# Gate blocks of a hybrid attention layer: bank copies on ScalarE in place of VectorE

## The chip, the cores and the metric

The kernel runs on one core of a Trainium2 chip. A core has a matmul engine (TensorE, "PE" in the profile, its weight loads "PEld"), VectorE ("DVE"), ScalarE ("ACT"), GpSimd ("POOL") and SyncE ("SP"). Each engine takes its instructions from its own queue in the order in which the program was built; semaphores make one engine wait for another. Matmul results land in PSUM, eight banks of 128 partitions by 512 float32 words, and have to be copied out of a bank by DVE or ACT before the bank can be written anew. The metric is the device time of one execution in microseconds (us), the median of several runs.

## The reference, cut to what matters

One layer of a streaming encoder over a prompt of 1024 tokens and a sample of 32 new tokens with 512 cached ones; the kernel handles both as 1056 columns. One projection of the normalised input gives everything that the two attention branches and their gates need:

```python
p = h @ w_in      # 1024 -> 384 + 256 + 32 + 3*512 + 1024 + 1024
q_lat, c_kv, k_r, q_b, k_b, v_b, g_a, g_b = jnp.split(p, IN_SPLITS, axis=-1)
...
def sb_attend(q, qpos, k, v, kpos):            # branch B, stick-breaking, 8 heads of 64
    z = jnp.einsum('bqhd,bshd->bhqs', q, k).astype(jnp.float32) * SB_SCALE
    mask = kpos[None, :] < qpos[:, None]
    sp = jnp.where(mask, jax.nn.softplus(z), 0.0)
    later = lax.cumsum(sp, axis=3, reverse=True) - sp
    a = jnp.where(mask, jnp.exp(jax.nn.log_sigmoid(z) - later), 0.0)
    return jnp.einsum('bhqs,bshd->bqhd', a.astype(v.dtype), v)
...
merged = (jax.nn.sigmoid(g_a) * (o_a @ w_proj_a)
          + jax.nn.sigmoid(g_b) * (o_b @ w_proj_b))
```

Branch A (latent attention with softmax), the output projection and a convolutional feed-forward block follow. The change concerns the projections `g_a` and `g_b`, 2 x 1024 columns, which are computed early, put away in DRAM, and read back when the two branches are merged.

## The kernel before

Products are kept at float32 accuracy by splitting each operand into a high part and a rest and adding three products (`mm3`, L66: the lines L68 to L70 are its matmuls, high by high, rest by high and high by rest as the profile names them). `hi` (L61, on ACT) makes the high part, `lo` (L64, on DVE) the rest. Weights are loaded by `wload` (L77, issued on SP) and split by `wsplit`.

The stage in question is `stage_sb`. It goes through four pairs of heads. For a pair, `sb_pair` projects queries, keys and values (`mtile`: a block of output columns, 352 at a time, is 24 matmuls into one bank), then runs `attend` for each of the two heads. After each pair, `gates` projects four of the sixteen gate blocks of 128 rows, each in three blocks of 352 columns. A gate block's bank (tag `mm`, two banks in turn) is copied to a tile `nat` (two buffers in turn), and GpSimd's queue issues the store to the DRAM tensor `gd` (L649). That makes 48 copies (L648) and 48 stores.

In `attend`, 128 rows of queries at a time go through a chain that changes engines often:

- PE: scores into one or two banks of tag `s`, three banks in turn (L462 to L466);
- `sb_weights`: ACT takes Abs, Exp and Ln of each piece (L481, L482, L483), DVE makes softplus (L484), then a scan along the row, which is the reversed running sum (L486), then subtracts it from the scores (L489), which frees the `s` banks; ACT takes the last Exp (L490);
- PE transposes the weights 128 by 128 into a bank `tr` (L542); ACT splits off the high part (L61, tiles `PTh` and `ptd`), DVE the rest (L64, `PTl` and `ptd`);
- PE multiplies them with the values into a bank `pv` (L555); ACT copies one half (L559), DVE adds the other (L560), and the result is stored (L564).

The gate matmuls do not depend on the attention around them. The order of the instructions on each engine is not the order in which the Python code issues them: the framework's scheduler lays it out when the program is built, from dependencies, free buffers and its own estimates of durations, and mixes gate matmuls between the steps of attention. On the chip this order is fixed. Between gate blocks there are also small products for the modulation vectors (`ada_step`, L199 and L203), which use the same two `mm` banks.

Of the kernel before, what the change touches and what calls it, by code (L numbers as in the profile page):

```python
# [40 lines left out]
class K:  # L41
# [598 lines left out]
    def gates(self, ms):  # L640
        nc = self.nc
        for m in ms:
            wh, wl = self.w_in_tile(2208 + m * P)
            if self.ada_todo:
                self.ada_step(2, self.W, self.At)
            for c0, n, ps in self.mtile(wh, wl, self.Hh, self.Hl, self.BLK, KT):
                g = self.tl(self.At, [P, 512], F32, "nat")
                nc.vector.tensor_copy(g[:, :n], ps[:, :n])  # L648
                nc.gpsimd.dma_start(self.gd[m, :, c0 : c0 + n], g[:, :n])  # L649

    def att_pools(self):
# [930 lines left out]
    def stage_down(self):  # L1582
# [57 lines left out]
        def product(banks, s, weights, first, more=None, part=range(6)):  # L1640
            for i, (j, n) in enumerate(steps):
                if i not in part:
                    continue
                wh, wl = weights(i, j, n)
                gh, gl = gates(s, j, n)
                if more:
                    more(i, j, n)
                for k in range(n):
                    for t in range(4):
                        tk = slice(t * P, t * P + P)  # L1650
                        add3(banks[t], gh[:, k, tk], gl[:, k, tk], wh[:, k], wl[:, k], first and j + k == 0, j + k == NJ - 1)
# [189 lines left out]
```

## Time and profile before

| | us |
|---|---|
| median of three runs | 1797.5 |
| the three runs | 1796.99, 1797.5, 1802.86 |
| the profiled execution | 1796.74 |
| its span in the profile | 1794.7 |
| PE busy | 1733.5 (97%) |
| PEld busy | 1547.7 (86%) |
| DVE busy | 1258.4 (70%) |
| ACT busy | 1005.4 (56%) |
| POOL busy | 253.3 (14%) |
| DVE, the 48 copies L648 | 24.5 |

How the rows of the profile are read. A row of a group gives the line, the engine, the operation, output<-input by the program's names, shapes, and a count. A row of waits reads "who, line <- who released it, line: us in total, times, longest". A row of a stretch of time gives start:end and length, then busy us and number of instructions of PE, PEld, DVE, ACT and POOL, then the granted clock of PE as a share of full speed, the share of the DMA engines that is busy, and GB/s. A row of the time line gives start and length in us, then the instruction (x2: two in a row merged), and in brackets the idle time before it with what ended it. Matmuls overlap: a matmul of 352 columns has a mean length of some 330 ns in the groups, while the next one starts well before its end.

### The profile page before, as it was taken

To read this page: it belongs to the slowest core of one execution; us is meant where nothing else is said; L and a number is where in the kernel's file an instruction comes from. 1 tells how busy PE (TensorE), PEld (TensorE's weight loads), DVE (VectorE), ACT (ScalarE), POOL (GpSimd) and SP (SyncE) were. 2 spreads that over 40 slices of the span, in tenths; PEclk is the share of its full clock that TensorE was granted. 3 is DMA by queue.
4 is the path that set the end of the run, shared out by engine and by line. 5 is a ranking of instruction groups with operands and counts; after the bars stand their busy time and mean duration, and the time that the engine had idled before them with its cause. 6 is when DMAs were issued, how large, how long until landed. Compare 5 with 4: busy or idle time off the path is not lost. (4 is left out here: it accounts for less than half of the span.)

```text
span 1794.7 us, 30062 instructions
## 1 busy us (share of the span) xinstructions
PE 1733.5 (97%) x11610; PEld 1547.7 (86%) x11610; DVE 1258.4 (70%) x2087; ACT 1005.4 (56%) x1926; POOL 253.3 (14%) x518
## 2 busy tenths in 40 slices
PE   6999999999999999999999999999999999999997
PEld 3988888988888998888888868999999999977876
DVE  4677377576487467777676768977777787788446
ACT  4565366564464469688687357644444454544332
POOL 2112111110111001101000022321111111110001
PEclk9999999999999999999999999999999999999999
DMA  8333332332333112313336542333333323597426
GB/s 316 109 101 106 101 100 74 90 111 83 101 103 85 57 54 77 90 51 95 101 115 218 169 154 83 124 124 124 101 124 126 132 90 124 196 344 260 147 87 224
DMA packets 181710, 227.52 MB, mean 127 GB/s; under 512 B 13349, under 2 KB 129776, under 8 KB 181568
## 3 DMA queue, kind: packets, MB, share of 16 engines
q1 hardware_dynamic: 166048, 182.10, 31.7%
q0 software_dynamic: 15296, 43.42, 6.8%
q8 instruction: 91, 1.49, 0.3%
q14 instruction: 51, 0.42, 0.1%
q10 hardware_dynamic: 224, 0.09, 0.0%
HBM read 174.32 MB, written 51.25 MB: 126 GB/s over the span
## 5 line engine op out<-in xcount | busy, mean ns | idle before, releaser
L61 ACT ACTIVATE wh<-wr 128x1024 fp32r<-128x1024 f32 (+6 forms) x185 | 149.5, 818 | 254.9 <-PE s L1305 83.4
L64 DVE TENSOR_TENSOR wl<-wr,wh 128x1024 fp32r<-128x1024 f32 (+6 forms) x185 | 168.3, 916 | 137.0 <-ACT wh L61 135.5
L68 PE MATMUL mm<-hh,wh 128*128 128x352 f32 x696 | 229.6, 330 | 2.4 <-DVE nat L648 2.4
L69 PE MATMUL mm<-hl,wh 128*128 128x352 f32 x696 | 228.6, 328 | 0.4 <-DVE hl L277 0.4
L70 PE MATMUL mm<-hh,wl 128*128 128x352 f32 x696 | 228.0, 328 | 0.0
L68 PEld LDWEIGHTS mm<-hh,wh 128*128 128x128 f32 x696 | 131.3, 189 | 10.3 <-issue 4.1
L69 PEld LDWEIGHTS mm<-hl,wh 128*128 128x128 f32 x696 | 131.5, 189 | 2.7 <-DVE hl L277 0.9
L70 PEld LDWEIGHTS mm<-hh,wl 128*128 128x128 f32 x696 | 131.6, 189 | 1.2 <-issue 0.4
L542 PE MATMUL tr<-c,A 128*128 128x128 f32 x576 | 93.7, 277 | 4.9 <-ACT A L490 3.6
L1306 PE MATMUL s<-T,wl 128*128 128x256 f32 (+1 forms) x328 | 93.4, 285 | 0.0
L1305 PE MATMUL s<-T,wh 128*128 128x256 f32 (+1 forms) x328 | 93.3, 285 | 0.0
L1304 PE MATMUL s<-T,wh 128*128 128x256 f32 (+1 forms) x328 | 93.3, 284 | 0.0
L486 DVE TENSOR_TENSOR_SCAN A<-A 128x128 f32<-128x128 f32 (+8 forms) x66 | 87.8, 1343 | 0.4
L1442 DVE SCALAR_TENSOR_TENSOR u<-u,c,u 128x1058 f32<-128x1058 f32 x68 | 87.0, 1316 | 1.4 <-ACT u L1439 0.2
L490 ACT ACTIVATE A<-A 128x128 f32<-128x128 f32 (+8 forms) x66 | 44.6, 682 | 74.8 <-DVE A L489 74.3
L64 DVE TENSOR_TENSOR PTl<-tr,PTh 128x512 fp32r<-128x512 f32 x96 | 62.9, 683 | 29.9 <-ACT PTh L61 29.5
L542 PEld LDWEIGHTS tr<-c,A 128*128 128x128 f32 x576 | 67.5, 141 | 14.4 <-ACT A L490 8.1
L1304 PE MATMUL tr<-T,wh 128*128 128x272 f32 (+1 forms) x272 | 77.7, 286 | 0.0
L1306 PE MATMUL tr<-T,wl 128*128 128x272 f32 (+1 forms) x272 | 77.4, 285 | 0.0
L1305 PE MATMUL tr<-T,wh 128*128 128x272 f32 (+1 forms) x272 | 77.3, 284 | 0.0
L64 DVE TENSOR_TENSOR wl<-S,wh 128x1024 fp32r<-128x1024 f32 x40 | 48.9, 1223 | 37.8 <-ACT wh L61 37.8
L1304 PE MATMUL mm<-T,wh 128*128 128x256 f32 (+1 forms) x256 | 73.1, 286 | 0.0
(650 smaller groups left out, 5557.1 us busy)
## 6 DMA issues: line engine op xcount, KB each, us to landing
wr<-in_w_ada_dram SPq DMA_DIRECT2D x48, 512.0 KB, 4.7
wr<-in_w_up_dram SPq DMA_DIRECT2D x44, 512.0 KB, 3.8
dr<-in_w_down_dram SPq DMA_DIRECT2D x43, 512.0 KB, 5.8
wr<-gdn SPq DMA_DIRECT2D x34, 512.0 KB, 3.9
wr<-in_w_in_dram SPq DMA_DIRECT2D x33, 512.0 KB, 4.2
gdn<-u POOLq DMA_DIRECT2D x23, 512.0 KB, 4.8
gd<-nat POOLq DMA_DIRECT2D x48, 176.0 KB, 2.1
t<-gd SPq DMA_DIRECT2D x16, 528.0 KB, 5.2
```

The source lines that it names most:

```text
L61: self.nc.scalar.activation(out, in_, AF.Identity, scale=scale)
L64: return self.nc.vector.tensor_tensor(out, full, hi.bitcast(F32), ALU.subtract)
L68: m(ps, lh, rh, start=start, stop=False)
L69: m(ps, lh, rl, start=False, stop=False)
L70: m(ps, ll, rh, start=False, stop=stop)
L486: nc.vector.tensor_tensor_scan(r, r, r, 0.0, ALU.add, ALU.bypass)
L490: nc.scalar.activation(A[:, :w], A[:, :w], AF.Exp)
L542: nc.tensor.transpose(tr[:, (2 * s + q) * P : (2 * s + q + 1) * P], at[q][:, b * P : b * P + P], self.idt)
L1304: m(ps[:, :n], w[0][:, k], x[0][:, k, c], start=first and k == 0, stop=False, skip_group_check=True)
L1305: m(ps[:, :n], w[0][:, k], x[1][:, k, c], start=False, stop=False, skip_group_check=True)
L1306: m(ps[:, :n], w[1][:, k], x[0][:, k, c], start=False, stop=k == 3, skip_group_check=True)
L1442: nc.vector.scalar_tensor_tensor(y, u[:, w : w + YW], self.cvT[:, w, cc : cc + 1], y, ALU.mult, ALU.add)
```

## The change

One line in `gates`: the copy of a gate block out of its bank is issued on ScalarE and no longer on VectorE. Shape, source, target and store stay the same. As the scheduler lays out the order anew, the built program also differs in the order of instructions on all five queues, from the first gate copies to the end of `stage_sb`; ahead of that and behind it the order is the same.

```diff
             for c0, n, ps in self.mtile(wh, wl, self.Hh, self.Hl, self.BLK, KT):
                 g = self.tl(self.At, [P, 512], F32, "nat")
-                nc.vector.tensor_copy(g[:, :n], ps[:, :n])
+                nc.scalar.copy(g[:, :n], ps[:, :n])
                 nc.gpsimd.dma_start(self.gd[m, :, c0 : c0 + n], g[:, :n])
```

## The prediction, made before the change was run

> **What bounds the kernel now.** I read the page first, then sums by stretch, then the waits of the matmul engine in the stretch that the change touches, and last its time line around single waits.
>
> ```profile
> span 1794.7 us, 30062 instructions
> PE 1733.5 (97%) x11610; PEld 1547.7 (86%) x11610; DVE 1258.4 (70%) x2087; ACT 1005.4 (56%) x1926; POOL 253.3 (14%) x518
> ...
> 60.00:561.00 501.00, 486.01 (x3189) 431.30 (x3188) 330.57 (x545) 285.99 (x593) 75.24 (x131) 1.00 0.32 97
> ...
> 60.00:80.00 20.00, 20.00 (x128) 19.70 (x127) 8.57 (x13) 8.68 (x16) 3.06 (x4) 1.00 0.26 80
> 260.00:280.00 20.00, 19.64 (x131) 17.90 (x129) 18.45 (x31) 15.21 (x33) 2.18 (x4) 1.00 0.33 103
> ```
>
> TensorE (PE) is busy 97% of the span. The gate copies run from 93 to 561 us, so the second part of the fence is the stage that counts: in its 501 us PE is busy 486.0, the granted clock is 1.00, VectorE (DVE) has 330.6 us of work and ScalarE (ACT) 286.0. PE idles 15.0 us there, 0.8% of the kernel. That is the most that any relief of the other engines can win, unless the matmuls themselves shrink, which they do not. The last row shows why the other engines still matter: where attention is dense, DVE is busy 18.45 of 20 us, ACT 15.21. The row above it gives the pace of the gate matmuls alone: 128 in 20 us, 0.156 us each, so a block of 24 takes 3.75 us.
>
> The 15 us of idle time, by what ended them:
>
> ```profile
> PE s L462 <- DVE A L489: 7.2, 20, 1.0
> PE tr L542 <- ACT A L490: 2.7, 5, 0.7
> PE mm L68 <- DVE nat L648: 2.4, 2, 1.2
> PE pv L555 <- DVE PTl L64: 1.2, 4, 0.4
> PE pv L555 <- ACT PTh L61: 1.1, 2, 0.9
> ...
> PEld s L462 <- DVE A L489: 10.7, 18, 0.8
> PEld tr L542 <- ACT A L490: 7.0, 15, 1.0
> ...
> ACT A L490 <- DVE A L489: 68.7, 27, 4.7
> DVE A L484 <- ACT A L483: 20.7, 22, 2.3
> ```
>
> All 33 waits sit in the chain of stick-breaking attention: scores (L462) wait for a bank that DVE's subtraction (L489) must leave, transposes (L542) wait for ACT's last Exp (L490), and twice a gate block waits for the gate copy itself (L648). In the last two rows the Exp waits for DVE far longer than DVE waits for ACT: in this chain DVE is the late one.
>
> **The change, part by part.** Removed from DVE and added to ACT are the same 48 copies of 128x352 out of PSUM. DVE's price has a row; ACT's comes from copies of the same shape from the same kind of bank that it does today.
>
> ```profile
> L648 DVE COPY nat<-mm x48: 496/511/525, 93.1 to 560.8; 128x352 f32<-128x352 f32 x48
> L446 ACT COPY big<-mm x12: 452/452/455, 73.4 to 469.2; 128x352 f32<-128x352 f32 x12
> L649 POOL DMA_DIRECT2D gd<-nat x48: 539/568/603, 93.9 to 561.6; - x48
> DMA to landing us min/median/max: 2.1/2.1/5.5
> ```
>
> DVE loses 48 x 0.510 = 24.5 us (330.6 becomes 306.1), ACT gains 48 x 0.452 = 21.7 us (286.0 becomes 307.7). Both stay some 193 us under the 501 of the stage, so neither becomes its bound, and these two terms add nothing by themselves. In ends and starts a copy costs DVE a little less, 0.42 us, since the next instruction starts before its end (below). The 48 stores stay on POOL's queue and follow the copy; POOL is busy 75 of 501 us, a store is issued in 0.57 us and lands in 2.1, 2.7 together, less than the 3.75 of a block, so the two copy buffers come free as before. A few stores of gates and of attention outputs change places on POOL's queue, and on SP's queue one cache load moves behind two weight loads; nobody on PE waits for these today, and I put them at nothing.
>
> In the built program the instructions are not only moved from one queue to the other: the scheduler lays the stage out anew. From the end of the stage on, all five queues are the same as before. So the effect is a matter of PE's waits between 60 and 561 us, and I go through them.
>
> Gain, first term: waits for the copy itself.
>
> ```profile
> 102.61 1.75 DVE L486 TENSOR_TENSOR_SCAN A<-A 128x768 f32<-128x768 f32 x1
> 104.27 0.50 DVE L648 COPY nat<-mm 128x352 f32<-128x352 f32 x1
> 104.68 1.01 DVE L489 TENSOR_TENSOR A<-s,A 128x384 f32<-128x384 f32 x2
> ...
> 104.82 0.43 PE L68 MATMUL mm<-hh,wh 128*128 128x352 f32 x1 [1.21 <-DVE nat L648]
> 366.24 0.43 PE L68 MATMUL mm<-hh,wh 128*128 128x352 f32 x1 [1.19 <-DVE nat L648]
> ...
> 105.73 0.85 ACT L490 ACTIVATE A<-A 128x768 f32<-128x768 f32 x1 [3.70 <-DVE A L489]
> ```
>
> The copy lay behind a scan of 1.75 us while ACT had nothing to do for 3.70 us. Both waits go: -1.21 - 1.19 = -2.4 us. What could be late next is the Exp of 0.85 us in ACT's queue, half a scan.
>
> Gain, second term: score matmuls that wait for L489 where a copy stood between the scan and L489. There are six, three of them repeated one for one in a later pair:
>
> ```profile
> 115.10 0.50 PE L462 MATMUL s<-KH,Q 128*128 128x512 f32 x1 [0.26 <-DVE A L489]
> 220.46 0.50 DVE L648 COPY nat<-mm 128x352 f32<-128x352 f32 x1
> 220.88 0.78 DVE L489 TENSOR_TENSOR A<-s,A 128x272 f32<-128x272 f32 x2
> 221.45 0.36 PE L462 MATMUL s<-KH,Q 128*128 128x256 f32 x1 [1.01 <-DVE A L489]
> 246.93 0.47 PE L462 MATMUL s<-KH,Q 128*128 128x448 f32 x1 [0.47 <-DVE A L489]
> 376.51 0.50 PE L462 MATMUL s<-KH,Q 128*128 128x512 f32 x1 [0.25 <-DVE A L489]
> 480.75 0.36 PE L462 MATMUL s<-KH,Q 128*128 128x256 f32 x1 [0.23 <-DVE A L489]
> 506.21 0.47 PE L462 MATMUL s<-KH,Q 128*128 128x448 f32 x1 [0.46 <-DVE A L489]
> ```
>
> The copy delays L489 by 0.42 us (220.46 to 220.88). Each wait shrinks by that at most: 0.26 + 0.42 + 0.42 + 0.25 + 0.23 + 0.42 = 2.0 us. Sum of gains -4.4 us.
>
> Loss, third term: the copies in ACT's queue. In the built order 18 of the 48 stand directly ahead of an Exp L490, 12 inside the Abs, Exp, Ln run (L481 to L483), 8 ahead of the small copy L559, the others beside weight splits. None follows an L490 directly, so none waits behind one that waits for DVE.
>
> ```profile
> L490 ACT ACTIVATE A<-A x65: 291/657/1061, 86.1 to 558.9; 128x128 f32<-128x128 f32 x8, 128x256 f32<-128x256 f32 x8, 128x384 f32<-128x384 f32 x8, 128x512 f32<-128x512 f32 x8
> L489 DVE TENSOR_TENSOR A<-s,A x98: 260/547/692, 85.8 to 558.2; 128x384 f32<-128x384 f32 x24, 128x512 f32<-128x512 f32 x22, 128x320 f32<-128x320 f32 x16, 128x448 f32<-128x448 f32 x16
> ```
>
> Of 65 Exps 27 wait for DVE, 2.5 us each in the mean, and cover a copy of 0.452. The other 38 would be pushed: 18 x 38/65 x 0.452 = 4.8 us of delay; 20 of 65 transposes stand right behind (5 waits on PE, 15 on its weight loads), so 4.8 x 20/65 = 1.5 us reach PE. Inside the run, 12 x 0.452 us count where DVE waits for L483 (22 of about 100 pieces) and then where a score waits for L489 (38 of 98): 0.5 us. The ends of this term are 0 (every copy in idle time) and 48 x 0.452 = 21.7 us (none); I stay near the low end, since the 68.7 us of Exps waiting are the row nearest to it. An end below 0 I exclude here: a lighter DVE is counted in the gains and in the second rival.
>
> ScalarE against VectorE for such a copy: the Trainium skill, page "ScalarE: Activation LUTs", section "Rules for kernel authors", sends simple arithmetic to VectorE and budgets about 0.3 us plus 0.83 ns per element for an ACTIVATE. By that budget a copy of 352 would take about 0.59 us (an estimate from the page), 48 of them 28.5 us, dearer than on VectorE, and the third term would grow by a third, to 2.6. The row of this trace says 0.452 against 0.510, the other way, so I do not use it.
>
> Sum: -2.4 - 2.0 + 1.5 + 0.5 = -2.4 us. The profiled execution took 1796.74 us (span 1794.7 and 2.0 around it) and lies 0.8 under the median of the three runs, 1797.5. So 1794.3 as a profiled execution, 1795.0 as a median.
>
> **The rivals.** Faster by more. DVE is the root of nearly all waits: L489 holds 7.2 us of them, the copy 2.4, and the Exps behind 2.7 wait for L489 in turn. With 24.5 of 330.6 us off DVE all 12.3 may go, less the 1.9 above: -10.4, 1787. For it speak the 18.45 of 20 us; against it, that the new order puts scores and transposes just behind their producers again.
>
> Slower. A copy in ACT's strictly ordered queue waits for its block's last matmul, and what stands behind it, the Exp or L559 on which PE's next step hangs, waits along. The 26 copies ahead of such a link (18 and 8), each in full, are 11.8 us; less the gain of 4.4 that is +7.4, 1805. It decides (over 0.3%) once 22 copies come uncovered: (5.4 + 4.4) / 0.452. For it: DVE's copies already waited 8 times for their block (9.5 us, row below). Against it: the Exps' 68.7 us of waiting.
>
> ```profile
> DVE nat L648 <- PE mm L70: 9.5, 8, 2.1
> ```
>
> The strict order itself is stated by the Trainium skill, "PSUM — Partial Sum Buffer", section "Engine vs sequencer instructions"; the trace agrees, as DVE's copies held their queue in those 8 places.
>
> Nothing gained. The new order merely trades waits. PE's idle time differs between pairs of heads with the same work:
>
> ```profile
> 60.00:190.00 130.00, 125.12 (x825) 112.42 (x824) 86.95 (x143) 73.94 (x150) 23.06 (x41) 1.00 0.33 100
> 450.00:580.00 130.00, 126.85 (x835) 111.78 (x834) 88.53 (x149) 72.07 (x152) 19.49 (x34) 1.00 0.30 92
> ```
>
> 4.9 us in the first pair's 130, 3.2 in the last's. If each of the four pairs shifts by half of that 1.7, the sum shifts by 3.5 either way; this gives the forecast its own range, 1791.5 to 1798.5, with "no change" in it.
>
> **How the numbers follow.** A run of this kernel can tell some 0.3% from no change, 5.4 us: under 1792.1 is faster, over 1802.9 slower. Forecast with its own range 0.5, of which 0.05 falls under 1792.1; faster rival 0.26; slower rival 0.24. So faster 0.31, same 0.45, slower 0.24. The range reaches to the faster rival, 1787, and to 1804, just short of the slower one.
>
> **What would show it.** Right: the waits of PE between 60 and 561 us sum to about 12 instead of 14.6, none of them for a gate copy; DVE near 306 and ACT near 308 us there; copies near 0.45 us; the stages after it as long as before. Wrong, to the slow side: transposes waiting for L490 or for PTh (L61) well above 2.7 and 1.1, or ACT idle at L648 for PE's blocks with L490 behind it. Wrong, to the fast side: scores waiting for L489 under 2 us. A later stage that changes length, or an ACT copy above 0.5 us, would break the argument itself.

## The result, and the profile after the change

The changed kernel took 1794.73 us in the median of 22 runs, the kernel before 1798.72 us in 22 runs beside it: a ratio of 0.9978, 95% interval 0.9968 to 0.9988. That is 0.22% less, inside the 0.3% that the prediction counts as no change, and 0.3 us from the predicted 1795.0. The number was right, in part by luck: the forecast was counted from three runs of the kernel before with a median of 1797.5, the later runs put that kernel at 1798.72, so the change is -4.0 us (2.2 to 5.8 by the interval) where -2.4 was forecast. The reason was not right.

Head of the page of the changed kernel, and a sum by stretch (start:end and length, then busy us of PE, PEld, DVE, ACT and POOL with counts, the granted clock, DMA share, GB/s):

```profile
span 1791.2 us, 30074 instructions
PE 1726.4 (96%) x11610; PEld 1545.9 (86%) x11610; DVE 1239.7 (69%) x2039; ACT 1023.0 (57%) x1974; POOL 254.9 (14%) x518
```

```profile
60.00:560.00 500.00, 481.64 (x3197) 431.57 (x3196) 314.69 (x499) 304.44 (x642) 75.39 (x131) 1.00 0.33 98
560.00:1791.20 1231.20, 1202.85 (x8119) 1085.65 (x8118) 892.74 (x1470) 687.92 (x1279) 167.22 (x359) 1.00 0.40 132
```

The work moved as the diff says: over 500 us of the stage DVE has 314.7 us of work (330.6 in 501 before) and ACT 304.4 (286.0). PE's matmuls are as many as before, 11610, yet PE is busy 7.1 us less in the whole span (1733.5 to 1726.4). The prediction had said that the matmuls do not shrink.

The waits of PE between 60 and 562 us, and below them waits of the other engines in the same stretch (who, line <- releaser: us in total, times, longest):

```profile
PE s L462 <- DVE A L489: 11.8, 28, 1.3
PE tr L542 <- ACT A L490: 3.3, 6, 0.7
PE mm L68 <- DVE ada L203: 2.2, 4, 0.5
PE pv L555 <- DVE PTl L64: 0.6, 3, 0.3
...
ACT A L490 <- DVE A L489: 46.6, 27, 3.1
DVE A L484 <- ACT A L483: 37.7, 29, 3.0
ACT nat L648 <- PE mm L70: 11.8, 16, 2.1
```

PE does not wait less. Its waits sum to 17.9 us, where they were 14.6. The two waits for a gate copy (2.4 us) are gone, but the score matmuls wait 11.8 us for DVE's subtraction L489, 7.2 before, and gate blocks wait 2.2 us for the addition L203 behind a modulation product, which they did not do at all. So less idle time cannot be the gain.

What shrank is one group of matmuls, the small products of `ada_step` (L199). There are 16 such products. Each fills a bank through 32-column tiles, in 8 matmuls as the code issues them, 16 in the trace. The group is given for the kernel before, then for the changed one (count | busy us, mean ns of one | idle):

```profile
L199 PE MATMUL mm<-wr,cT 128*32 128x256 f32 x256 | 26.6, 389 | 0.0
```

```profile
L199 PE MATMUL mm<-wr,cT 128*32 128x256 f32 x256 | 21.6, 387 | 0.0
```

The same 256 matmuls with the same mean length take 5.0 us less together. The time line of PE shows how. Before, one product is cut into three pieces of 2, 8 and 6 by attention's matmuls:

```profile
150.18 0.62 PE L199 MATMUL mm<-wr,cT 128*32 128x256 f32 x2
150.73 0.88 PE L542 MATMUL tr<-c,A 128*128 128x128 f32 x6
151.53 0.64 PE L199 MATMUL mm<-wr,cT 128*32 128x256 f32 x8
152.10 0.39 PE L555 MATMUL pv<-PTh,V 128*128 128x256 f32 x1
152.42 0.63 PE L199 MATMUL mm<-wr,cT 128*32 128x256 f32 x6
152.98 0.43 PE L68 MATMUL mm<-hh,wh 128*128 128x352 f32 x1
```

After the change the same product runs in one piece:

```profile
146.55 0.32 PE L70 MATMUL mm<-hh,wl 128*128 128x352 f32 x1
146.80 1.07 PE L199 MATMUL mm<-wr,cT 128*32 128x256 f32 x16
147.80 0.43 PE L68 MATMUL mm<-hh,wh 128*128 128x352 f32 x1
```

Whole, the 16 matmuls hold PE from 146.80 to 147.80. In three pieces they hold it from 150.18 to 150.73, 151.53 to 152.10 and 152.42 to 152.98: 0.55 + 0.57 + 0.56 = 1.68 us. A piece of 2 costs as much as a piece of 8. The starts of the single matmuls, which the merged rows above do not show, give the reason. In the whole product the 16 start in four groups of four, the four of a group within 0.02 us: at 146.80, 147.04, 147.26 and 147.47. In the pieces of 2, 8 and 6 there are six groups, of 1 and 1, of 4 and 4, and of 3 and 3. From group to group it is 0.22 to 0.24 us, whether one matmul is in it or four, and from the last matmul of a piece to the next other matmul 0.31. A cut here therefore costs twice: it splits groups of four that start together in the whole product, and it adds one more change to other matmuls. Counted over the stage, the 16 products lie in 38 unbroken runs before and in 26 after.

So after the first comparison there were two theories. **Relief**: the gain comes from the lighter DVE, as predicted, and the shrunken L199 is beside the point. **Order**: the gain comes from the order in which the scheduler laid out PE's matmuls around the new copies, above all from fewer broken runs; which engine copies makes no odds.

### The profile page after: what moved, and what is told of

Its sections match the earlier page's. It is cut to its first block, busy times and chain, and to the rows that moved or that the text cites. A ratio compares the mean times of both kernels' runs of the same rounds, so it can differ in the third digit from the quotient of the medians.

```text
span 1791.2 us, 30074 instructions
## 1 busy us (share of the span) xinstructions
PE 1726.4 (96%) x11610; PEld 1545.9 (86%) x11610; DVE 1239.7 (69%) x2039; ACT 1023.0 (57%) x1974; POOL 254.9 (14%) x518
## 5 line engine op out<-in xcount | busy, mean ns | idle before, releaser
L68 PEld LDWEIGHTS mm<-hh,wh 128*128 128x128 f32 x696 | 131.5, 189 | 10.4 <-DVE ada L203 4.1
L484 DVE SCALAR_TENSOR_TENSOR A<-s,A 128x384 f32<-128x384 f32 (+5 forms) x100 | 52.2, 545 | 37.9 <-ACT A L483 37.7
```

The source lines that it names most:

```text
L68: m(ps, lh, rh, start=start, stop=False)
L484: nc.vector.scalar_tensor_tensor(A[:, c], ps[:, :n], 0.0, A[:, c], ALU.max, ALU.add)
```

## The experiments

To compare the kernels I use, beside the timed runs, the stretch of one profiled execution between the same two matmuls, the 481st of PE and the 8000th from its end. Ahead of it and behind it the order is the same in the changed kernel and in the one before. "Idle" is the stretch less PE's busy time.

| kernel | stretch us | PE busy | PE idle | runs of L199 | L199 busy | ratio of times, 95% |
|---|---|---|---|---|---|---|
| before | 493.4 | 477.6 | 15.8 | 38 | 26.55 | 1 |
| changed | 491.1 | 472.0 | 19.1 | 26 | 21.63 | 0.9978 (0.9968 to 0.9988) |
| e1 VectorE, order of the changed kernel | 495.8 | 472.3 | 23.5 | 26 | 21.63 | 1.0022 (1.0010 to 1.0034) |
| e2 ScalarE, order of the kernel before | 495.1 | 477.0 | 18.1 | 38 | 26.55 | 1.0013 (1.0003 to 1.0023) |
| e3 VectorE, whole runs | 487.9 | 469.6 | 18.3 | 16 | 17.13 | 0.9973 (0.9959 to 0.9986) |
| e4 ScalarE, whole runs | 488.1 | 468.5 | 19.6 | 16 | 17.13 | 0.9977 (0.9966 to 0.9989) |
| e5 ScalarE, runs split | 494.3 | 480.1 | 14.2 | 44 | 29.01 | 1.0016 (1.0005 to 1.0027) |

The rows of the stretch, of the kernel before and of the changed one:

```profile
87.30:580.70 493.40, 477.56 (x3132) 423.47 (x3130) 331.99 (x543) 277.64 (x570) 70.92 (x125) 1.00 0.31 96
87.20:578.30 491.10, 472.05 (x3132) 422.70 (x3130) 313.18 (x495) 294.70 (x618) 71.05 (x125) 1.00 0.33 97
```

### The two orders, each with the other engine

The order of PE's matmuls in the stage is written out from the one kernel and forced on the other. The added dependencies fix only the order of issue; they add no wait on the chip. The queues of the other engines are laid out anew around it; no run forces a kernel's own order on it unchanged, so what this alone does to the time is not measured. e1 is the kernel before (copies on VectorE) with the changed kernel's order:

```diff
+        self.pin()
+
+    def pin(self):
+        byname = {i.name: i for i in self.nc.cur_bb.bb.instructions}
+        seq = [byname[f"I-{x}"] for x in PE_ORDER.split()]
+        for a, b in zip(seq, seq[1:]):
+            self.tc.add_manual_dep(b, a.name, mybir.DependencyInfo(mybir.DependencyClass.NoSync, mybir.DependencyReason.DATA), reason="pe_order")
+PE_ORDER = """
...
+"""
```

> The copies stay on VectorE, but TensorE's queue is pinned to the order that it has in the changed kernel (the other queues are laid out anew around it). Theory 'order': the 3.5 us between the two profiles come from the modulation matmuls (L199), which the new order breaks into 26 runs instead of 38, 21.6 us busy instead of 26.6; the kernel is then as fast as the changed one, 0.22% (4 us) under before, with L199 at 21.6 us. Theory 'relief' (the one of the prediction): VectorE's load is what counts, so the kernel stays within 1 us of before.

Measured: 1799.68 us against 1796.53 for the kernel before beside it, ratio 1.0022 (1.0010 to 1.0034). Its row for the stretch, and PE's waits between 60 and 580 us:

```profile
87.30:583.10 495.80, 472.32 (x3133) 423.47 (x3131) 333.65 (x543) 278.75 (x570) 70.87 (x125) 1.00 0.32 96
```

```profile
PE s L462 <- DVE A L489: 10.5, 15, 1.8
PE mm L68 <- DVE nat L648: 5.1, 4, 1.5
```

Both theories miss here. The order brought its shorter matmuls, as "order" says (PE busy 472.3, L199 21.63), but no gain: PE idles 23.5 us, 7.7 more than in the kernel before. The two rows hold 15.6 of it, where the same two waits were 9.6 before (7.2 and 2.4). The order was laid out for copies on ScalarE; with DVE copying, a gate block now waits four times for its bank, 5.1 us in all. Part of the stretch's length is chance: in this execution alone of those in the table PE's granted clock fell to half for 3.4 us of the stretch (from 533.05), which lengthens it by 1.7 us at most (an estimate from those 3.4 us). The idle time of the two rows does not come from it, and the 12 timed runs show no gain either. So the order alone does not make the gain. It has to fit the engines too: at this one order of the matmuls the ratio to the kernel before is 0.9978 with ScalarE copying and 1.0022 with VectorE (measured on two chips), and "which engine copies makes no odds" is wrong there.

e2 is the reverse, the changed kernel with the order of the kernel before (the same edit, the other list):

```diff
                 g = self.tl(self.At, [P, 512], F32, "nat")
-                nc.vector.tensor_copy(g[:, :n], ps[:, :n])
+                nc.scalar.copy(g[:, :n], ps[:, :n])
...
+        self.pin()
```

> The copies go to ScalarE, but TensorE's queue is pinned to the order that it has in the kernel before. Theory 'order': no gain from L199 (26.6 us, 38 runs), time within 2 us of before or a little over it, as scores and transposes are placed for the other engine. Theory 'relief': with the same order of matmuls the waits for the copy (2.4 us) go and the six waits behind L489 shrink by 2.0, so 2.4 to 4.4 us under before, and PE's waits between 60 and 561 us at 10 to 12 us instead of 14.6.

Measured: 1798.07 us, ratio 1.0013 (1.0003 to 1.0023) on the same chip. The stretch and PE's waits between 60 and 580 us:

```profile
90.10:585.20 495.10, 476.95 (x3132) 423.41 (x3130) 311.74 (x495) 294.76 (x618) 71.03 (x125) 1.00 0.31 96
```

```profile
PE s L462 <- DVE A L489: 10.0, 18, 1.1
PE pv L555 <- DVE ptd L64: 1.8, 3, 0.8
PE tr L542 <- ACT A L490: 1.6, 3, 0.9
PE mm L68 <- DVE ada L203: 1.1, 2, 0.6
```

This is the most direct test of the relief. PE's order is that of the kernel before, matmul by matmul; DVE has 311.7 us of work in the stretch where the kernel before has 332.0. With relief the kernel should be 2.4 to 4.4 us faster. It is 0.13% slower, and PE idles 18.1 us, 2.3 more. The waits for the gate copy are gone, and the scores wait 10.0 us where they waited 7.2. At this order of the matmuls the lighter DVE brings nothing.

### Whole runs, with either engine

If broken runs are what costs, gathering them should help whichever engine copies. e3 and e4 are the kernel before and the changed kernel, each with its own order, in which all matmuls of a product are moved to the place of its last part. The edit is that of e1, each with the list of its own kernel rewritten by that rule; of e3:

```diff
 PE_ORDER = """
...
-1636 1147 1148 1149 1174 1175 1176 1186 1187 1188 1637 1638 1639 1642 1083 1084 1085 1096 1097 1098 1643 1644 1645
+1147 1148 1149 1174 1175 1176 1186 1187 1188 1083 1084 1085 1096 1097 1098 1636 1637 1638 1639 1642 1643 1644 1645
...
 """
```

The numbers are the program's names of the matmuls. 1636 to 1645 are the eight of the product whose pieces of 2, 8 and 6 stand above.

> The kernel before, TensorE's order pinned to its own, only that each of the 16 modulation products (16 matmuls L199) stands in one run, at the place of its last part. Theory 'order': 38 runs become 16; at the 0.41 us per run that the step from 38 to 26 brought (4.9 us), some 9 us under before (0.5%), L199 busy near 17.5 us. Theory 'relief': no change within 2 us, since VectorE has the same work.

> The changed kernel with the same edit: TensorE's order pinned to its own, each modulation product in one run. Theory 'order': 26 runs become 16, 4 us under the changed kernel, 8 us under before, and no faster than the same edit with the copies on VectorE. Theory 'relief': as the changed kernel, 4 us under before, and 4 us under the same edit on VectorE.

Measured on the chip of e1 and e2: e3 1791.33 us, 0.9973 (0.9959 to 0.9986); e4 1792.50 us, 0.9977 (0.9966 to 0.9989). The stretch of e3, then of e4:

```profile
88.70:576.60 487.90, 469.63 (x3133) 422.69 (x3131) 332.89 (x543) 278.42 (x570) 70.94 (x125) 1.00 0.32 97
```

```profile
88.30:576.40 488.10, 468.49 (x3132) 422.04 (x3129) 312.77 (x495) 295.18 (x618) 71.00 (x125) 1.00 0.32 97
```

The group L199 of e3 (that of e4 has the same numbers):

```profile
L199 PE MATMUL mm<-wr,cT 128*32 128x256 f32 x256 | 17.1, 385 | 0.0
```

With the copies still on VectorE, gathering the runs gives as much as the whole change did, and with the runs gathered the engine makes no difference that the runs can tell: 487.9 and 488.1 us for the stretch, while DVE has 332.9 us of work in the one and 312.8 in the other. From before to e3 the runs fall by 22 and L199 by 26.55 - 17.13 = 9.4 us, 0.43 us a run; PE's whole busy time falls by 7.9, 0.36 a run; of this 2.5 went into idle time (15.8 to 18.3). Both gains are smaller than was expected. e3 was to lie some 9 us under before and lies 5.2 under it; e4 was to lie 4 us under the changed kernel, and its ratio (0.9977) is that of the changed kernel (0.9978), though its stretch is 3.0 us shorter (491.1 to 488.1).

### The changed kernel with its runs broken again

e5 is the changed kernel in its own order, with nine of its products cut into three parts of 1, 4 and 3 matmuls as the code issues them, one other matmul between the parts. Nothing else changes in PE's order; the other queues are again laid out around it.

```diff
 PE_ORDER = """
...
-1532 1533 1534 1535 1538 1539 1540 1541 1544 1545
+1532 1544 1533 1534 1535 1538 1545 1539 1540 1541
...
 """
```

> The changed kernel with TensorE's order pinned to its own, but nine of its modulation products that stood whole are cut into three parts with one other matmul between the parts, as the kernel before has them: 43 runs where the changed kernel has 26. Theory 'order': each run more costs 0.43 us (26.55 - 17.13 us of L199 over 38 - 16 runs), so L199 is busy 29 us in place of 21.6, and the kernel is 7 us over the changed one, 3 us over before (0.2%), with PE's idle time as in the changed kernel. Theory 'relief': as the changed kernel, 4 us under before, since ScalarE and VectorE do the same.

Measured on another chip: 1798.25 us against 1795.91 for the kernel before beside it, 1.0016 (1.0005 to 1.0027). The runs came to 44. Stretch and group:

```profile
87.40:581.70 494.30, 480.07 (x3133) 422.99 (x3131) 313.05 (x495) 295.90 (x618) 71.25 (x125) 1.00 0.32 96
```

```profile
L199 PE MATMUL mm<-wr,cT 128*32 128x256 f32 x256 | 29.0, 390 | 0.0
```

18 more runs than the changed kernel: L199 +7.4 us (0.41 a run), PE's busy time +8.0, the stretch +3.2, and the gain is gone, though DVE is as light as in the changed kernel (313 us). The idle time was expected to stay as in the changed kernel; it fell by 4.8 us (19.1 to 14.2 in the table), so more than half of the added busy time came out of waits. The 0.16% over before is close to the 0.2% that was expected. Undoing the order takes the gain away; e3 and e4 give it without the change of engine.

### The products taken out of the stage

The other way to test it: no L199 in the stage at all. e6 (VectorE) and e7 (ScalarE) issue the modulation products in `proj_b`, a later stage, so that there are no runs to break.

```diff
             wh, wl = self.w_in_tile(2208 + m * P)
-            if self.ada_todo:
-                self.ada_step(2, self.W, self.At)
...
         for m in range(KT):
+            if m % 2 == 0:
+                self.ada_step(2, self.W, self.At)
```

> Copies on VectorE as before, the order left to the scheduler, but the 16 modulation products are no longer mixed into the gate blocks: they stand in proj_b of the latent attention. Reference for the next run; against before open (their cost moves to another stage), between 8 us faster and 4 us slower. Stage_sb gets shorter by about the 27 us that L199 was busy there, under either theory.

> The same with the copies on ScalarE. Theory 'order': with no L199 in the stage ScalarE has nothing to win there: no faster than the same kernel with the copies on VectorE, and up to 3 us slower, by the idle time that the change added (15.8 to 19.1 us). Theory 'relief': still 4 us faster than the same kernel with the copies on VectorE.

Measured: 1823.33 us, 1.0152 (1.0132 to 1.0171), and 1825.28 us, 1.0181 (1.0155 to 1.0206). As whole kernels they are 27 and 29 us over before, where e6 was expected at most 4 over. The loss lies behind the stage: from its end to the end of the kernel e6 takes 1244.2 us where the kernel before takes 1187.2, with PE busy 36.5 us longer, 27.3 of it with the products themselves, and idle 20.5 us longer. One part of that idle time is the products' wait for their weights (a row of PE's waits in e6; then 350 us of the later part, columns as above); the rest of the loss was not followed up:

```profile
PE mm L199 <- DMA wr<-in_w_ada_dram: 5.7, 4, 2.6
```

```profile
550.00:900.00 350.00, 324.29 (x2163) 274.83 (x2161) 206.70 (x486) 219.34 (x502) 34.74 (x62) 0.99 0.33 99
```

PE is busy 324 of 350 us there. The stage itself still answers the question: measured from the first matmul of L389 to the first of L763 (L761 in e6 and e7, whose edit shifts the lines), it takes 539.3 us before, 537.0 in the changed kernel, 512.7 in e6 and 512.5 in e7, the last two with 16.0 and 17.7 us of idle time. Without the products, the two engines give the same length, from one execution each, each in the order that the scheduler gave it.

### The changed kernel and both kernels with whole runs on one chip

e8 is the changed kernel without an edit, e9 is e3 and e10 is e4 again, so that the three stand beside the same runs of the kernel before.

> The changed kernel again, beside the next two on one chip, since its first measurement was made elsewhere. Both theories: 0.2% under before.

> The kernel before with whole runs again. Theory 'order': below the changed kernel, by the 3.2 us that its stretch of stage_sb is shorter in the profile (487.8 against 491.1), so about 0.35 to 0.4% under before. Theory 'relief': 0.2% or more above the changed kernel.

> The changed kernel with whole runs again. Theory 'order': within 1 us of the same edit on VectorE (488.2 against 487.8 in the profiles), 2 to 3 us under the changed kernel. Theory 'relief': as the changed kernel and 4 us under the same edit on VectorE.

| kernel | median us | ratio to before (1796.85), 95% | stretch us | PE busy | PE idle |
|---|---|---|---|---|---|
| e8 changed | 1794.28 | 0.9988 (0.9972 to 1.0004) | 489.8 | 471.6 | 18.2 |
| e9 VectorE, whole runs | 1792.71 | 0.9979 (0.9967 to 0.9990) | 487.5 | 469.5 | 18.0 |
| e10 ScalarE, whole runs | 1792.69 | 0.9978 (0.9966 to 0.9989) | 490.7 | 468.9 | 21.8 |

Between the two kernels with whole runs the engine makes no difference again (1792.71, 1792.69). The changed kernel, expected 0.2% under before, came out 0.12% under it, with an interval that reaches past 1: on this chip its gain is not shown. Whole runs lie 1.6 us under the changed kernel, less than expected, and the intervals overlap: they are the best version found, about 0.2% under the kernel before, but not shown to beat the changed kernel. e10's stretch, 490.7 where the same kernel had 488.1 as e4, shows how far two executions of one kernel differ: 2.6 us.

## Why the prediction was right and wrong, by its steps

**The two terms that "add nothing by themselves".** Right: the copies take what they were priced at, by the group's row of the changed kernel (shortest/median/longest ns):

```profile
L648 ACT COPY nat<-mm x48: 430/452/476, 91.3 to 559.4; 128x352 f32<-128x352 f32 x48
```

0.452 us, as taken from L446. The load that went over was mis-sized, though: between the same two matmuls DVE's busy time fell by 18.8 us (332.0 to 313.2) and ACT's rose by 17.1 (277.6 to 294.7), not by 24.5 and 21.7. The rows of neighbouring instructions overlap, as the 0.42 us from a copy's start to the next start already said, so 48 row lengths are more than 48 copies add. The budget of the Trainium skill ("ScalarE: Activation LUTs", section "Rules for kernel authors") had given an estimate of 0.59 us; that row is for an ACTIVATE with a pointer operand as bias, and the measurement decides against it for these copies.

**Gain, first term (-2.4 us).** Right as far as it goes: PE no longer waits for a gate copy.

**Gain, second term (-2.0 us).** Wrong. The six score waits were to shrink with the copy gone from between scan and subtraction; the waits of L462 for L489 rose from 7.2 to 11.8 us. One place shows why a copy's 0.42 us cannot be taken off a wait. These rows of the changed kernel are the place that the prediction quotes at 220 to 221 us:

```profile
216.72 1.29 DVE L486 TENSOR_TENSOR_SCAN A<-A 128x544 f32<-128x544 f32 x1
218.05 0.79 DVE L489 TENSOR_TENSOR A<-s,A 128x272 f32<-128x272 f32 x2
218.63 0.36 PE L462 MATMUL s<-KH,Q 128*128 128x256 f32 x1 [1.28 <-DVE A L489]
```

The copy no longer stands between the scan and L489, and the score still waits 1.28 us, 1.01 before. By subtraction, PE ran out of other matmuls 218.63 - 1.28 - 216.72 = 0.63 us after the start of the scan. Before, that was 1.19 us: the scan of the kernel before starts at 219.25 (row below), and the score at 221.45 had waited 1.01.

```profile
219.25 1.29 DVE L486 TENSOR_TENSOR_SCAN A<-A 128x544 f32<-128x544 f32 x1
```

The new order left PE without other work 0.56 us earlier. DVE came 0.30 us sooner to L489 (1.33 us after the scan's start, 1.63 before), so the wait grew by 0.27. A wait on PE measures the order against the chain, and the order is not a constant of the change.

**Loss, third term (+2.0 us).** Its parts cannot be read one by one. The transposes' waits for L490 rose by 0.6 us (2.7 to 3.3), the named 1.5 being the estimate. The side that was not priced is in the rows of the chain: ACT's Exp waits for DVE 46.6 us, 68.7 before, and DVE waits for ACT's Ln 37.7 us, 20.7 before. The two engines work in turns on one chain, and what the one was relieved of came back as waiting for the other: 89.4 us of such waits before, 84.3 after. In e2, with PE's order held, PE's idle time rose by 2.3 us; that this return is the cause of it is an inference from these rows and was not tested alone. Another candidate stands beside it: in e2 ACT's copies wait 18 times, 19.8 us in all, for their block's last matmul and hold ACT's queue meanwhile, and 11 of these times an Exp L490 is the next instruction.

**The sum.** -2.4 us was predicted, and -2.3 us is what the profiled stretch shows (493.4 to 491.1), but it is made of -5.5 us of busy time and +3.2 us of idle time. The agreement is chance. Nor need the idle time come from the new engine: e3, with the old one, has 2.5 us more of it for 7.9 us less of busy time. The step that failed is the premise in the reading of the bound: that 15 us of idle time is the most that can be won "unless the matmuls themselves shrink, which they do not". They did, by 12 runs at 0.41 us. The rest of the difference of the two profiled spans (3.5 us) lies behind the stretch, where the order is the same (1214.0 to 1212.9 us), and is taken as spread between executions.

**The rivals.** The faster one (-10.4 us by relief) is refuted by e2, e3 with e4, and e9 with e10; ScalarE wins only at the order that was laid out for it (0.9978 against the 1.0022 of e1). The slower one asked for 22 uncovered copies ahead of the chain. ACT's copies did wait for their blocks 16 times, 11.8 us, 10 of these times with an L490 next in the queue, which is the sign that the prediction named for the slow side. PE's waits for ACT do not grow by more than the 0.6 us named above, so it stayed without a price on PE. "Nothing gained" came nearest in its mechanism: waits were traded, +3.3 us on PE (14.6 to 17.9), inside the 3.5 either way that it priced from the spread between pairs of heads. It too counted idle time alone.

**"What would show it."** Copies of 0.45 us and the later stages hold. ACT near 308 (304.4 in 500 us) holds roughly; DVE near 306 does not (314.7), by the overlap named above. The waits of PE, 17.9 us where about 12 was asked, broke it: that line was the right one to check, and it said at once that the forecast was right for another reason.

What stays open: why the scheduler breaks fewer runs when the copies are on ScalarE. The result is seen in the order (ten of the sixteen products whole, four before); its cause was not tried. Nor was it tried to cut a product only between two groups of four.

## What to carry to other kernels

Where a scheduler lays out the order, moving work between two side engines is also a new order on the engine that bounds the kernel: compare that engine's busy time by group first, and only then its waits. Before believing a small gain, force the old order on the new kernel and the new order on the old one; here that separated a relief worth nothing at the old order from 5.5 us of shorter busy time. Busy time saved is not time saved: from 44 runs to 16 (e5 to e4) PE's busy time falls by 0.41 us a run and the stretch by 0.22, as the idle time grows by the difference. Small column-tiled products should be issued without other matmuls between their parts: that gave the same 0.2% (e3, e9) with no engine changed.

## What the runs showed of the hardware that was not expected

The cost of a run of 32-column matmuls goes by its groups of matmuls that start together, and not by their number: pieces of 2, 8 and 6, two groups each, took 0.62, 0.64 and 0.63 us, and 16 in one run, four groups, 1.07. The ends of matmuls in these rows are modelled; from start to next start it is 0.55, 0.57, 0.56 and 1.00 us. Over four layouts the same 256 matmuls were busy 17.13 us in 16 runs, 21.63 in 26, 26.55 in 38 and 29.01 in 44, 0.41 to 0.45 us for each further run. In groups that start together these are 64, 76, 88 and 94, which is 0.38 to 0.41 us for each further group.

The Trainium skill ("TensorEngine Tiling (Array Packing)", section "PSUM Bottleneck") advises to use both ScalarE and VectorE to clear PSUM behind tiled matmuls. The copies moved here stand behind full-width matmuls, and both engines empty banks in this stage already; moving 48 more of them from one to the other brought nothing at equal order of the matmuls (e2, 1.0013).
